# Operands laid out transposed by numpy before the launch, and a new division of U blocks among the stages of a two-layer decoder trunk

## The chip, the cores and the metric

One core of a Trainium2 chip runs the whole program in one launch. The metric is the device time of that launch in microseconds (us). What numpy does to the inputs before the launch is not in the time. The engines are TensorE (PE, with its weight loads shown as PEld), VectorE (DVE), ScalarE (ACT), GpSimd (POOL) and SyncE (SP), which here only issues DMAs.

## What is computed

Two layers (DEPTH 2) over 512 tokens of width 1024. Each layer is a mixing sub-layer (stick-breaking attention, mLSTM, spatial gating) and then a retrieval of experts, which takes most of the time:

```python
q = matmul(xt, wq).reshape(t, 8, 2, 128)
scores = einsum('thcd,hcnd->thcn', q, sub_keys)         # 2 x 128 keys for each of 8 heads
sv, si = top_k(scores, 16)                              # then the 16 best of the 16 x 16 sums: idx, gate
act = einsum('td,thkd->thk', xb, u_tab[idx])            # u_tab: 16384 x 1024
y = einsum('thk,thkd->td', gelu(act) * gate, v_tab[idx])
```

The spatial gating multiplies by `w_s * tril`, four 128x128 matrices in a layer.

## The kernel before, in words

For the first 384 tokens (TD) the kernel doesn't gather experts: it computes the gelu of the products of all 16384 rows of U with the tokens, multiplies by a dense matrix of gates, and multiplies by all rows of V. The tables go through in 128 blocks of 128 rows: a U block e, a V block k. The last 128 tokens are gathered row by row: 256 indirect DMAs of 512 KB in a layer (`gather_u`, `gather_v`), each followed by one DVE product. Every fp32 operand is split in two parts of type fp32r (`u_hi` and `u_lo`, `v_hi` and `v_lo`, `wh` and `wl`), and each product takes three matmuls.

Stages of a layer, in order of time:

1. Front: `mixing` and `peer_front` (L618). For each of 16 pairs of head and half, `peer_front` loads the keys `kr`, turns them on PE (L648), copies them to `kt` on ACT (L650), and multiplies. `sg_all` (L537) turns its four matrices on PE in the same way (L550).
2. Selection: `stage2` (L803) for four tiles of tokens, nearly all of it on DVE.
3. One-hot: `onehots` (L895) builds the dense gates from one-hot products: DVE writes `oeq` (L907) and `oag` (L911), PE multiplies them (L917), ACT evacuates (L920), and a DMA stores them in DRAM (`gd`).
4. Tail: the U blocks left until V may begin.
5. V: for each k of 128, load (`vload`), split (`vprep`) and multiply (`vmm`, 18 matmuls of 512 columns, L997); the other U blocks lie among these.

A U block is 24 matmuls of 384 columns (`uact`, L738), then a gelu on ACT (L741). Before it, `uload` (L683) brings 512 KB of U rows through SP's queue and `utrans` (L693) makes the transposed halves, in one of two ways. In the stages selection and one-hot, eight PE transposes into two PSUM tiles T (L711), then for each tile an ACT copy to `u_hi` (L713) and a DVE subtraction to `u_lo` (L714). From the tail on, for blocks e of at least `u_tail + 3` (L1000), the rows come in four DMAs of 128 KB arranged in 32x32 squares, DVE turns them in one instruction (L702), and then follow one ACT copy (L705) and one DVE subtraction (L706). The tiles `u_hi` and `u_lo` have two buffers each, so block e + 1 is prepared while block e is multiplied, in the buffers of block e - 1; `u_raw` has three.

What divides the U blocks: `paced` (L925) takes the steps of selections and one-hot products, adds a credit for each step (W_S = 1.0 for each of 27 selection steps, W_O / 2 = 0.25 for each of 96 one-hot steps), and emits one U block (`uphase`, L745) for each whole credit. 27 + 24 = 51 blocks are emitted so. The tail takes e from 51 to UB + 2 = 62, 12 blocks, and the V loop the other 65, spread over its first 120 steps (`u_on`). The results of the first NS = 52 blocks are stored in DRAM (`ge`) and read back before their V block (`gelu_r`); later ones stay in NB = 11 buffers. One gather is emitted for every second one-hot step (48), one for each tail block, and the rest are spread over the V loop.

The tail and the V loop lie in a `manual_schedule` block: there each engine's order is the order of the code. Elsewhere a scheduler with a cost model of its own fixes each engine's order when the program is built.

Of the kernel before, what the change touches and what calls it, by code (L numbers as in the profile page):

```python
# [7 lines left out]
F32 = mybir.dt.float32  # L8
F32R = mybir.dt.float32r
# [3 lines left out]
AF = mybir.ActivationFunctionType  # L13
# [4 lines left out]
P = 128  # L18
S = 512
NT = S // P  # L20
D = 1024
ND = D // P
# [10 lines left out]
NK = 128  # L33
# [8 lines left out]
NCH = TD // TC  # L42
GE = 4
GPAD = 128
NB = 11
NS = 52
UB = NS + NB - 3
W_S = 1.0
W_O = 0.5
G_R = 1  # L50
G_B = 1
DVT = 0
UDV = []
GBUF = 4
UEND = 120
LOG_EXP = "natural_log_exp_and_others"
# [12 lines left out]
@with_exitstack  # L69
def trunk_kernel(ctx: ExitStack, tc: tile.TileContext, x, norm1_g, w_in, sb_qn_g, sb_kn_g, ml_conv_w,  # L70
                 ml_conv_b, ml_i_b, ml_f_b, sg_vn_g, sg_w, sg_b, out_g, w_out, norm2_g, peer_wq,
                 peer_keys, peer_u, peer_v, out):
    nc = tc.nc
    depth = w_in.shape[0]

# [4 lines left out]
    ident = consts.tile([P, P], F32, name="ident")  # L80
# [109 lines left out]
    def blocked(ap):  # L190
        return ap.rearrange("p (f c) -> p c f", c=ND)
# [56 lines left out]
    def mixing(l, wst, fr, at, ps):  # L248
# [3 lines left out]
        with ExitStack() as yctx:  # L252
# [284 lines left out]
            def sg_all():  # L537
                sq = tmp("e", 1)[:, :NT * WG].rearrange("p (t g d) -> p t g d", t=NT, d=HD)
                nc.vector.tensor_mul(sq, vv, vv)
                r = small.tile([P, NT, GS], F32, name="sgr")  # L540
                nc.vector.tensor_reduce(r, sq, op=ALU.add, axis=AX.X)
                rsqrt_mean(r, r, HD)
                nc.vector.tensor_mul(vv, vv, r[:, :, :, None].to_broadcast([P, NT, GS, HD]))
                for t in range(NT):
                    nc.vector.tensor_mul(vv[:, t], vv[:, t], vn.rearrange("p (g d) -> p g d", d=HD))
                for g in range(GS):
                    wr = tmp("dg", 2, (P, NT, P))[:, 0, :]
                    nc.sync.dma_start(wr, sg_w[l, g])
                    pw = ps.tile([P, S], F32, name="tr", bufs=1)
                    nc.tensor.transpose(pw[:, :P], wr, ident)  # L550
                    wt = tmp("dg", 2, (P, NT, P))[:, 0, :]
                    nc.vector.tensor_mul(wt, pw[:, :P], upper)
                    pg = ps.tile([P, S], F32, name="tr", bufs=1)
                    pg4 = pg[:, :NT * HD].rearrange("p (t d) -> p t d", d=HD)
                    nc.tensor.matmul(pg4, wt, vv[:, :, g, :], start=True, stop=True)
                    ug = uu[:, :, g * HD:(g + 1) * HD]
                    nc.vector.scalar_tensor_tensor(ug, pg4, col("sgb", g), ug, op0=ALU.add, op1=ALU.mult)
                    sum_sq(ug, rsg[:, :, g])
# [59 lines left out]
    def peer_front(l, pctx, mctx, at, wst, ps, pools, uload):  # L618
# [17 lines left out]
        with ExitStack() as fctx:  # L636
            fr = fctx.enter_context(tc.tile_pool(name="pf", bufs=1, side="right"))
            for c0 in range(0, 2 * PH, 3):
                n = min(3, 2 * PH - c0)
                wn = load_split(wst, peer_wq[l], (c0 + 3) * P, min(3, 2 * PH - c0 - 3) * P,  # L640
                                perm=True) if c0 + 3 < 2 * PH else None
                for c in range(n):
                    hc = c0 + c
                    h, which = hc // 2, hc % 2
                    kr = fr.tile([P, P], F32, name="kr", bufs=2)
                    nc.sync.dma_start(kr, peer_keys[l, h, which])
                    pk = ps.tile([P, S], F32, name="zz", bufs=4)
                    nc.tensor.transpose(pk[:, :P], kr, ident)  # L648
                    kt = fr.tile([P, P], F32, name="kt", bufs=2)
                    nc.scalar.activation(kt, pk[:, :P], AF.Copy)  # L650
                    pt = ps.tile([P, S], F32, name="mm", bufs=2)
                    lh = lambda a, d: a[:, d, c * P:(c + 1) * P]
                    for t0, t1 in ((0, TD), (TD, S)) if hc < 2 else ((0, S),):
# [20 lines left out]

    def layer(l):
        with ExitStack() as pctx:
            pools = {"dvt": set(UDV)}
            uraw, uT, vraw, vT, wT, g4 = {}, {}, {}, {}, {}, {}

            def dve_t(e):  # L680
                return e in pools["dvt"]

            def uload(e):  # L683
                if e < NK and dve_t(e):
                    uraw[e] = pools["up"].tile([P, 4, ND * 32], F32, name="u_raw", bufs=3)
                    rows = peer_u[l, e * NK:(e + 1) * NK, :].rearrange("(g b) (a c) -> a b g c", b=32, a=4)
                    for a in range(4):
                        nc.sync.dma_start(uraw[e][32 * a:32 * (a + 1)], rows[a])
                elif e < NK:
                    uraw[e] = pools["up"].tile([P, D], F32, name="u_raw", bufs=3)  # L690
                    nc.sync.dma_start(uraw[e], peer_u[l, e * NK:(e + 1) * NK, :])

            def utrans(e, half, ps, tag="T", **kw):  # L693
                if e >= NK:
                    return
                if half == 0:
                    uT[e] = (pools["up"].tile([P, ND, P], F32R, name="u_hi"), pools["up"].tile([P, ND, P], F32R, name="u_lo"))
                uh, ul = uT[e]
                if dve_t(e):
                    if half == 0:  # L700
                        uraw[e], src = pools["up"].tile([P, ND, P], F32, name="u_t", bufs=1), uraw[e]
                        nc.vector.transpose(uraw[e].rearrange("p c (g b) -> p g c b", g=4),  # L702
                                            src.rearrange("p g (f c) -> p g c f", f=32))
                    else:
                        nc.scalar.activation(uh, uraw[e], AF.Copy)  # L705
                        nc.vector.tensor_sub(ul, uraw[e], uh.bitcast(F32))  # L706
                    return
                pt = ps.tile([P, S], F32, name=tag, **kw)
                d0 = half * 4
                for d in range(4):  # L710
                    nc.tensor.transpose(pt[:, d * P:(d + 1) * P], blocked(uraw[e])[:, d0 + d], ident)  # L711
                p3 = pt.rearrange("p (d e) -> p d e", e=P)
                nc.scalar.activation(uh[:, d0:d0 + 4, :], p3, AF.Copy)  # L713
                nc.vector.tensor_sub(ul[:, d0:d0 + 4, :], p3, uh[:, d0:d0 + 4, :].bitcast(F32))  # L714

            with ExitStack() as fctx:
                ps = fctx.enter_context(tc.tile_pool(name="ps_f", bufs=1, space=PSUM))
                wst = fctx.enter_context(tc.tile_pool(name="wst", bufs=1))
                mctx = ExitStack()
                fr = mctx.enter_context(tc.tile_pool(name="fr", bufs=1))  # L720
                at = mctx.enter_context(tc.tile_pool(name="at", bufs=1))
                mixing(l, wst, fr, at, ps)
                pr, xg, sbuf, svs, sis = peer_front(l, pctx, mctx, at, wst, ps, pools, uload)
                for half in range(2):
                    utrans(0, half, ps, "y", bufs=1)
            dr = pctx.enter_context(tc.tile_pool(name="dr", bufs=1, space=bass.MemoryType.DRAM))
            gd = dr.tile([NCH, P, NK * TC + GPAD], F32, name="gd")
            ge = dr.tile([NS, P, TD], F32, name="ge")
# [16 lines left out]
            def uphase(e, ps):  # L745
                if e:
                    uload(e + 2)
                utrans(e + 1, 0, ps)
                utrans(e + 1, 1, ps)
                uact(e, ps)  # L750

            idx = pr.tile([P, PH * K], I32, name="idx")
# [191 lines left out]
            with ExitStack() as cctx:  # L944
# [52 lines left out]
                                nc.tensor.matmul(ya[2 * t + half], a[:, tsl], b[:, hs],  # L997
                                                 start=(k == 0 and i == 0), stop=(k == NK - 1 and i == 2))

                pools["dvt"].update(range(u_tail + 3 + DVT, NK))  # L1000
                with tc.manual_schedule():
                    uload(u_tail + 2)
                    for n, e in enumerate(range(u_tail, UB + 3)):
                        uload(e + 3)
                        utrans(e + 1, 0, ps, f"y{2 * n % 6}")
                        utrans(e + 1, 1, ps, f"y{(2 * n + 1) % 6}")
                        gather(G_R)
                        uact(e, ps, bufs=2)
                        if e >= UB + 1:
                            vload(e - UB - 1)  # L1010
                    ya += [ps.tile([P, D // 2], F32, name=f"y{i}") for i in range(2 * (NT - 1))]
                    vprep(0)
                    eu = UB + 3
                    for k in range(NK):
                        u_on = eu < NK and (k + 1) * (NK - NS - NB) >= (eu - NS - NB + 1) * UEND
                        vload(k + 2)
                        if u_on:
                            uload(eu + 3)
                            utrans(eu + 1, 0, ps)
                        vprep(k + 1)  # L1020
                        spread(2 * k, 252)
                        if u_on:
                            uact(eu, ps, bufs=2)
                            utrans(eu + 1, 1, ps)
                            eu += 1
                        vmm(k)
                        spread(2 * k + 1, 252)
# [8 lines left out]
    for t in range(NT):  # L1036
# [1 line left out]


_INS = ["x", "norm1_g", "w_in", "sb_qn_g", "sb_kn_g", "ml_conv_w", "ml_conv_b", "ml_i_b", "ml_f_b",  # L1040
        "sg_vn_g", "sg_w", "sg_b", "out_g", "w_out", "norm2_g", "peer_wq", "peer_keys", "peer_u", "peer_v"]
_OUTS = [((1, S, D), "float32")]


# [21 lines left out]
```

## Time and profile before

| | us |
|---|---|
| median of 3 runs | 3360.24 |
| lowest, highest | 3348.55, 3373.12 |
| the profiled execution | 3358.58 |
| its span, first to last instruction | 3356.9 |
| PE, PEld, DVE, ACT, POOL busy | 3237.4, 2875.2, 2792.9, 1395.2, 652.1 |

The profile is one execution. Busy time is the union of an engine's instructions. Matmuls overlap in the profile (one of 384 columns is shown as 340 ns and the next starts sooner than that), so what PE does in a stretch is read from the starts of its instructions, not from their lengths.

### The profile page before, as it was taken

To read this page: it belongs to the slowest core of one execution; us is meant where nothing else is said; L and a number is where in the kernel's file an instruction comes from. 1 tells how busy PE (TensorE), PEld (TensorE's weight loads), DVE (VectorE), ACT (ScalarE), POOL (GpSimd) and SP (SyncE) were. 2 spreads that over 40 slices of the span, in tenths; PEclk is the share of its full clock that TensorE was granted. 3 is DMA by queue.
4 is the path that set the end of the run, shared out by engine and by line. 5 is a ranking of instruction groups with operands and counts; after the bars stand their busy time and mean duration, and the time that the engine had idled before them with its cause. 6 is when DMAs were issued, how large, how long until landed. Compare 5 with 4: busy or idle time off the path is not lost.

```text
span 3356.9 us, 49064 instructions
## 1 busy us (share of the span) xinstructions
PE 3237.4 (96%) x18400; PEld 2875.2 (86%) x18400; DVE 2792.9 (83%) x4911; ACT 1395.2 (42%) x2142; POOL 652.1 (19%) x563
## 2 busy tenths in 40 slices
PE   8999999999999999999989999999999999999999
PEld 8787899898888888888887778889988888888888
DVE  4757898997888888988847578989978888989888
ACT  4554333664333333333355533336643333333333
POOL 1000003111232232223200000032112222332232
PEclk9999999999999999999999999999999999999999
DMA  4212137777999999999732121377779999999997
GB/s 136 72 33 90 56 121 273 265 282 230 279 296 291 283 292 291 304 297 290 246 112 66 32 90 55 121 271 265 282 233 282 296 289 289 302 301 302 286 290 255
DMA packets 388687, 742.40 MB, mean 221 GB/s; under 512 B 32996, under 2 KB 269600, under 8 KB 385376
## 3 DMA queue, kind: packets, MB, share of 16 engines
q1 hardware_dynamic: 295264, 398.64, 43.1%
q0 software_dynamic: 74752, 269.84, 25.4%
q10 hardware_dynamic: 18432, 70.79, 5.3%
q8 instruction: 144, 2.36, 0.3%
q14 instruction: 95, 0.78, 0.1%
HBM read 666.26 MB, written 72.88 MB: 220 GB/s over the span
## 4 chain that ended last, share of the span: by engine, by line
PE 65%; DVE 13%; DMA 11%; issue 5%; ACT 4%; POOL 1%; SPq 0%; ACTq 0%; DVEq 0%; POOLq 0%
PE y L997 22%; PE act L738 17%; PE mm L187 12%; DMA v_raw<-in_peer_v_dram 8%; PE oh L917 3%; PE mm L533 3%; DVE u_lo L714 2%; DMA u_raw<-in_peer_u_dram 1%; DVE u_t L702 1%; PE T L711 1%; PE zz L367 1%; PE zz L659 1%; PE zz L467 1%; PE y L478 1%; PE y L400 1%
## 5 line engine op out<-in xcount | busy, mean ns | idle before, releaser
L738 PE MATMUL act<-xh,u_lo 128*128 128x384 f32 x2048 | 698.1, 341 | 19.4 <-DVE u_lo L706 19.4
L738 PE MATMUL act<-xh,u_hi 128*128 128x384 f32 x2048 | 705.8, 345 | 11.1 <-ACT u_hi L705 10.7
L738 PE MATMUL act<-xl,u_hi 128*128 128x384 f32 x2048 | 696.7, 340 | 0.0
L997 PE MATMUL y<-v_hi,wh 128*128 128x512 f32 x1536 | 600.0, 391 | 8.8 <-ACT wh L984 8.8
L997 PE MATMUL y<-v_lo,wh 128*128 128x512 f32 x1536 | 600.2, 391 | 1.3 <-DVE v_lo L985 1.2
L997 PE MATMUL y<-v_hi,wl 128*128 128x512 f32 x1536 | 599.2, 390 | 0.0
L983 ACT ACTIVATE v_hi<-v_raw 128x1024 fp32r<-128x1024 f32 x256 | 272.0, 1062 | 742.6 <-DMA v_raw<-in_peer_v_dram 336.0
L985 DVE TENSOR_TENSOR v_lo<-v_raw,v_hi 128x1024 fp32r<-128x1024 f32 x256 | 313.1, 1223 | 146.4 <-ACT v_hi L983 146.2
L738 PEld LDWEIGHTS act<-xh,u_lo 128*128 128x128 f32 x2048 | 388.2, 190 | 26.8 <-DVE u_lo L706 26.8
L738 PEld LDWEIGHTS act<-xh,u_hi 128*128 128x128 f32 x2048 | 388.7, 190 | 24.8 <-ACT u_hi L705 17.3
L738 PEld LDWEIGHTS act<-xl,u_hi 128*128 128x128 f32 x2048 | 388.3, 190 | 4.8
L997 PEld LDWEIGHTS y<-v_hi,wh 128*128 128x128 f32 x1536 | 288.9, 188 | 65.8 <-ACT wh L984 10.7
L997 PEld LDWEIGHTS y<-v_hi,wl 128*128 128x128 f32 x1536 | 289.1, 188 | 62.5 <-DVE wl L986 1.5
L997 PEld LDWEIGHTS y<-v_lo,wh 128*128 128x128 f32 x1536 | 289.0, 188 | 58.0 <-DVE v_lo L985 2.9
L702 DVE STREAM_TRANSPOSE u_t<-u_raw 128x1024 f32<-128x1024 f32 x148 | 327.9, 2215 | 0.1
L765 POOL DMA_INDIRECT rows<-in_peer_u_dram,idx x128 | 150.3, 1174 | 788.1 <-DVE rows L768 412.7
L765 POOL DMA_INDIRECT sbuf<-in_peer_u_dram,idx x128 | 147.8, 1154 | 590.4 <-DVE sbuf L768 468.4
L741 ACT ACTIVATE gelu<-act 128x384 f32<-128x384 f32 x256 | 124.3, 485 | 299.7 <-PE act L738 298.7
L776 POOL DMA_INDIRECT rows<-in_peer_v_dram,idx x128 | 172.4, 1347 | 380.7 <-DVE x_sb L779 355.9
L984 ACT ACTIVATE wh<-wf 128x384 fp32r<-128x384 f32 x256 | 132.7, 518 | 244.9 <-DVE wf L980 244.0
L776 POOL DMA_INDIRECT sbuf<-in_peer_v_dram,idx x128 | 163.5, 1277 | 337.0 <-DVE x_sb L779 313.8
L706 DVE TENSOR_TENSOR u_lo<-u_t,u_hi 128x1024 fp32r<-128x1024 f32 x148 | 181.2, 1224 | 55.5 <-ACT u_hi L705 55.1
(309 smaller groups left out, 5890.1 us busy)
## 6 DMA issues: line engine op xcount, KB each, us to landing
v_raw<-in_peer_v_dram SPq DMA_DIRECT2D x256, 512.0 KB, 12.0
u_raw<-in_peer_u_dram SPq DMA_DIRECT2D x592, 128.0 KB, 11.5
u_raw<-in_peer_u_dram SPq DMA_DIRECT2D x108, 512.0 KB, 4.2
gd<-st ACTq DMA_DIRECT2D x24, 2048.0 KB, 7.3
gt<-gd SPq DMA_DIRECT2D x64, 768.0 KB, 14.0
w_raw<-in_w_in_dram SPq DMA_DIRECT2D x28, 768.0 KB, 4.5
ge<-gelu ACTq DMA_DIRECT2D x104, 192.0 KB, 4.4
gelu_r<-ge SPq DMA_DIRECT2D x104, 192.0 KB, 10.4
```

The costliest lines, as they stand in the source:

```text
L187: nc.tensor.matmul(ps, a_sel(a[ah], d), b_sel(b[bh], d), start=(d == 0 and i == 0), stop=(d == n - 1 and i == 2))
L533: nc.tensor.matmul(pt, yT[ah][:, b, t * P:(t + 1) * P], wo[bh][:, b, hs], start=(b == 0 and m == 0), stop=(b == n - 1 and m == 2))
L702: nc.vector.transpose(uraw[e].rearrange("p c (g b) -> p g c b", g=4), src.rearrange("p g (f c) -> p g c f", f=32))
L706: nc.vector.tensor_sub(ul, uraw[e], uh.bitcast(F32))
L738: nc.tensor.matmul(pa[:, :TD], a[:, d, :], b[:, d, :TD], start=(d == 0 and i == 0), stop=(d == ND - 1 and i == 2))
L741: nc.scalar.activation(gelu[e], pa[:, :TD], AF.Gelu_apprx_tanh)
L765: nc.gpsimd.indirect_dma_start(out=r, out_offset=None, in_=u_rows, in_offset=bass.IndirectOffsetOnAxis(ap=idx[:, p:p + 1], axis=0))
L776: nc.gpsimd.indirect_dma_start(out=r, out_offset=None, in_=v_rows, in_offset=bass.IndirectOffsetOnAxis(ap=idx[:, p:p + 1], axis=0))
L983: nc.scalar.activation(vh, vraw[e], AF.Copy)
L984: nc.scalar.activation(wh, wf, AF.Copy)
L985: nc.vector.tensor_sub(vl, vraw.pop(e), vh.bitcast(F32))
L997: nc.tensor.matmul(ya[2 * t + half], a[:, tsl], b[:, hs], start=(k == 0 and i == 0), stop=(k == NK - 1 and i == 2))
```

## The change

Numpy lays out three inputs before the launch: the four `sg_w` matrices and the keys transposed, and a further input `peer_ut` with each block of U transposed, 4 KB in a row for each partition. `utrans` with both its ways is replaced by `uprep`: one load, one ACT copy and one DVE subtraction for a block, from SBUF. The credits are 1.25 and 0.375, so that 33.75 + 36 = 69.75 are given out and 69 whole blocks are emitted among selections and one-hot products (the bound UB is 70), 4 in the tail (e from 69 to 72) and 55 in the V loop. NS is 60, NB is 13. `peer_u` stays for the gathers.

```diff
-NB = 11
-NS = 52
+NB = 13
+NS = 60
 UB = NS + NB - 3
-W_S = 1.0
-W_O = 0.5
+W_S = 1.25
+W_O = 0.75
...
                     nc.sync.dma_start(wr, sg_w[l, g])
-                    pw = ps.tile([P, S], F32, name="tr", bufs=1)
-                    nc.tensor.transpose(pw[:, :P], wr, ident)
                     wt = tmp("dg", 2, (P, NT, P))[:, 0, :]
-                    nc.vector.tensor_mul(wt, pw[:, :P], upper)
+                    nc.vector.tensor_mul(wt, wr, upper)
...
-                    kr = fr.tile([P, P], F32, name="kr", bufs=2)
-                    nc.sync.dma_start(kr, peer_keys[l, h, which])
-                    pk = ps.tile([P, S], F32, name="zz", bufs=4)
-                    nc.tensor.transpose(pk[:, :P], kr, ident)
-                    kt = fr.tile([P, P], F32, name="kt", bufs=2)
-                    nc.scalar.activation(kt, pk[:, :P], AF.Copy)
+                    kt = fr.tile([P, P], F32, name="kt", bufs=3)
+                    nc.sync.dma_start(kt, peer_keys[l, h, which])
...
-            def utrans(e, half, ps, tag="T", **kw):
...
+            def uload(e):
+                if e < NK:
+                    uraw[e] = pools["up"].tile([P, ND, P], F32, name="u_raw", bufs=3)
+                    nc.sync.dma_start(uraw[e], peer_ut[l, e])
+
+            def uprep(e):
+                if e < NK:
+                    uh = pools["up"].tile([P, ND, P], F32R, name="u_hi")
+                    ul = pools["up"].tile([P, ND, P], F32R, name="u_lo")
+                    src = uraw.pop(e)
+                    nc.scalar.activation(uh, src, AF.Copy)
+                    nc.vector.tensor_sub(ul, src, uh.bitcast(F32))
+                    uT[e] = (uh, ul)
...
             def uphase(e, ps):
                 if e:
                     uload(e + 2)
-                utrans(e + 1, 0, ps)
-                utrans(e + 1, 1, ps)
+                uprep(e + 1)
                 uact(e, ps)
...
                         uload(e + 3)
-                        utrans(e + 1, 0, ps, f"y{2 * n % 6}")
-                        utrans(e + 1, 1, ps, f"y{(2 * n + 1) % 6}")
+                        uprep(e + 1)
                         gather(G_R)
                         uact(e, ps, bufs=2)
...
                             uload(eu + 3)
-                            utrans(eu + 1, 0, ps)
                         vprep(k + 1)
                         spread(2 * k, 252)
                         if u_on:
                             uact(eu, ps, bufs=2)
-                            utrans(eu + 1, 1, ps)
+                            uprep(eu + 1)
                             eu += 1
...
+    inputs["sg_w"] = _np.swapaxes(inputs["sg_w"], 2, 3)
+    inputs["peer_keys"] = _np.swapaxes(inputs["peer_keys"], 3, 4)
+    u = _np.asarray(inputs["peer_u"])
+    inputs["peer_ut"] = u.reshape(u.shape[0], NK, NK, P, ND).transpose(0, 1, 3, 4, 2)
```

## Rows read from the trace of the kernel before

**Rows 1.** The page's first part, all of the span: busy us, share of the span and number of instructions of each engine.

```profile
PE 3237.4 (96%) x18400; PEld 2875.2 (86%) x18400; DVE 2792.9 (83%) x4911; ACT 1395.2 (42%) x2142; POOL 652.1 (19%) x563
```

**Rows 2.** Busy time in stretches: from and to in us from the span's start, length, then busy us and number of instructions of PE, PEld, DVE, ACT and POOL, the granted TensorE clock (1.00 is full speed), the busy share of the DMA engines and GB/s. In order: selection, one-hot, tail and V of the first layer, and V of the second.

```profile
438.00:596.00 158.00, 149.00 (x901) 144.35 (x900) 147.15 (x537) 57.98 (x97) 35.25 (x32) 0.99 0.67 229
596.00:788.00 192.00, 187.53 (x1860) 177.70 (x1861) 185.41 (x205) 128.31 (x161) 28.63 (x21) 0.99 0.75 266
788.00:861.00 73.00, 61.85 (x341) 56.39 (x338) 51.99 (x52) 22.87 (x34) 11.15 (x12) 1.00 0.78 221
861.00:1676.00 815.00, 803.63 (x3863) 707.90 (x3864) 717.38 (x781) 283.07 (x384) 243.78 (x194) 0.99 1.03 289
...
2541.00:3357.00 816.00, 803.89 (x3864) 709.99 (x3863) 718.12 (x782) 284.67 (x384) 240.30 (x192) 0.99 1.02 291
```

**Rows 3.** Groups of PE instructions in the selection, 438 to 596 us: line, operation, out<-in, sizes, number | busy us, mean ns of one | idle time before them and what ended it.

```profile
L738 PE MATMUL act<-xh,u_hi 128*128 128x384 f32 x223 | 78.0, 350 | 0.0
...
L711 PE MATMUL T<-ident,u_raw 128*128 128x128 f32 x224 | 32.7, 284 | 8.7 <-DVE u_lo L714 7.8 <-ACT sc L662 0.7
```

**Rows 4.** The same in the one-hot stage, 596 to 788 us.

```profile
L917 PE MATMUL oh<-oag,oeq 128*128 128x128 bf16 x1151 | 79.1, 221 | 4.6 <-DVE oag L911 3.3 <-ACT st L920 0.8
L738 PE MATMUL act<-xh,u_hi 128*128 128x384 f32 x177 | 62.0, 350 | 0.2 <-ACT u_hi L713 0.2
```

**Rows 5.** The same in the tail, 788 to 861 us.

```profile
L738 PE MATMUL act<-xh,u_hi 128*128 128x384 f32 x104 | 36.0, 346 | 2.1 <-ACT u_hi L705 2.1
```

**Rows 6.** The same in V, 861 to 1676 us.

```profile
L997 PE MATMUL y<-v_hi,wh 128*128 128x512 f32 x768 | 300.1, 391 | 5.1 <-ACT wh L984 5.1
...
L738 PE MATMUL act<-xh,u_lo 128*128 128x384 f32 x520 | 176.4, 339 | 6.3 <-DVE u_lo L706 6.3
L738 PE MATMUL act<-xh,u_hi 128*128 128x384 f32 x520 | 176.3, 339 | 2.8 <-ACT u_hi L705 2.8
```

**Rows 7.** PE in order of time in V: start us, us, engine, line, operation, out<-in, sizes, number. The first matmul of a V block, of the U block behind it, and of the next V block.

```profile
1004.10 0.40 PE L997 MATMUL y<-v_hi,wh 128*128 128x512 f32 x1
...
1008.19 0.34 PE L738 MATMUL act<-xh,u_hi 128*128 128x384 f32 x1
...
1012.38 0.40 PE L997 MATMUL y<-v_hi,wh 128*128 128x512 f32 x1
```

**Rows 8.** The same in the selection: the first matmul of a U block, the eight transposes behind it, and the first of the next U block.

```profile
547.66 0.42 PE L738 MATMUL act<-xh,u_hi 128*128 128x384 f32 x1
...
551.92 1.06 PE L711 MATMUL T<-ident,u_raw 128*128 128x128 f32 x8
552.73 0.42 PE L738 MATMUL act<-xh,u_hi 128*128 128x384 f32 x1
```

**Rows 9.** The same in the one-hot stage: 42 one-hot matmuls and what follows them.

```profile
671.88 2.79 PE L917 MATMUL oh<-oag,oeq 128*128 128x128 bf16 x42
674.47 0.42 PE L738 MATMUL act<-xh,u_hi 128*128 128x384 f32 x1
```

**Rows 10.** The same in the front: the transpose of one set of keys.

```profile
338.73 0.27 PE L648 MATMUL zz<-ident,kr 128*128 128x128 f32 x1
```

**Rows 11.** DVE in order of time in the tail, one round; in brackets idle time and what ended it.

```profile
825.86 2.19 DVE L702 STREAM_TRANSPOSE u_t<-u_raw 128x1024 f32<-128x1024 f32 x1
829.24 1.22 DVE L706 TENSOR_TENSOR u_lo<-u_t,u_hi 128x1024 fp32r<-128x1024 f32 x1 [1.19 <-ACT u_hi L705]
830.38 1.22 DVE L768 SCALAR_TENSOR_TENSOR rows<-rows,xg 128x1024 f32<-128x1024 f32 x1
...
831.52 2.18 DVE L702 STREAM_TRANSPOSE u_t<-u_raw 128x1024 f32<-128x1024 f32 x1
```

**Rows 12.** PE where the tail ends: the first matmul of V, and in brackets what it waited for.

```profile
860.96 0.50 PE L997 MATMUL y<-v_hi,wh 128*128 128x512 f32 x1 [3.74 <-ACT wh L984]
```

**Rows 13.** Groups of instructions over all of the span, columns as in rows 3.

```profile
L706 DVE TENSOR_TENSOR u_lo<-u_t,u_hi 128x1024 fp32r<-128x1024 f32 x148 | 181.2, 1224 | 55.5 <-ACT u_hi L705 55.1
...
L911 DVE TENSOR_TENSOR oag<-oeq,gateT 128x2048 bf16<-128x2048 bf16 x144 | 171.3, 1217 | 2.2 <-PE oh L917 2.2
...
L705 ACT ACTIVATE u_hi<-u_t 128x1024 fp32r<-128x1024 f32 x148 | 155.7, 1052 | 71.3 <-DVE u_t L702 71.3
...
L741 ACT ACTIVATE gelu<-act 128x384 f32<-128x384 f32 x256 | 124.3, 485 | 299.7 <-PE act L738 298.7 <-ACT st L920 0.8
...
L859 DVE TENSOR_TENSOR eq<-abb,iota_ak 128x4096 bf16<-128x4096 bf16 x8 | 18.3, 2290 | 0.0
```

**Rows 14.** Busy time and number of line 714 alone (the subtraction behind a PE transpose) in the selection and the one-hot stage: length, DVE busy.

```profile
438.00:596.00 158.00, 35.06 (x55) 0.99 0.67 229
596.00:788.00 192.00, 29.68 (x46) 0.99 0.75 266
```

**Rows 15.** DMA in V, 861 to 1676 us: GB/s in 40 slices of the stretch, packets and bytes, and two kinds of issue with their number, KB each and median us from issue to landing.

```profile
GB/s 287 319 277 293 312 287 302 273 292 285 297 285 286 305 265 268 296 296 331 284 303 287 282 295 289 296 314 295 298 302 301 291 297 304 271 285 318 264 271 152
DMA packets 137409, 235.43 MB, mean 289 GB/s; under 512 B 10420, under 2 KB 96440, under 8 KB 137355
...
v_raw<-in_peer_v_dram SPq DMA_DIRECT2D x125, 512.0 KB, 12.4
u_raw<-in_peer_u_dram SPq DMA_DIRECT2D x248, 128.0 KB, 12.2
```

**Rows 16.** Who waited for whom in V, longest in total first: us in total, times, longest us.

```profile
ACT v_hi L983 <- DMA v_raw<-in_peer_v_dram: 210.5, 51, 9.2
```

More of the change, by code (lines that the diff above doesn't have):

```diff
@@ L44 @@
 GPAD = 128
-NB = 11
-NS = 52
+NB = 13
+NS = 60
 UB = NS + NB - 3
-W_S = 1.0
-W_O = 0.5
+W_S = 1.25
+W_O = 0.75
 G_R = 1
 G_B = 1
-DVT = 0
-UDV = []
 GBUF = 4
@@ L71, in trunk_kernel @@
                  ml_conv_b, ml_i_b, ml_f_b, sg_vn_g, sg_w, sg_b, out_g, w_out, norm2_g, peer_wq,
-                 peer_keys, peer_u, peer_v, out):
+                 peer_keys, peer_u, peer_v, peer_ut, out):
     nc = tc.nc
@@ L676, in layer @@
         with ExitStack() as pctx:
-            pools = {"dvt": set(UDV)}
+            pools = {}
             uraw, uT, vraw, vT, wT, g4 = {}, {}, {}, {}, {}, {}
-            def dve_t(e):
-                return e in pools["dvt"]
             def uload(e):
[L684 to L691, printed above, removed]
@@ L693, in utrans @@
-            def utrans(e, half, ps, tag="T", **kw):
[L694 to L714, printed above, removed]
@@ L723, in layer @@
                 pr, xg, sbuf, svs, sis = peer_front(l, pctx, mctx, at, wst, ps, pools, uload)
-                for half in range(2):
-                    utrans(0, half, ps, "y", bufs=1)
+                uprep(0)
             dr = pctx.enter_context(tc.tile_pool(name="dr", bufs=1, space=bass.MemoryType.DRAM))
@@ L998, in vmm @@
                                                  start=(k == 0 and i == 0), stop=(k == NK - 1 and i == 2))
-                pools["dvt"].update(range(u_tail + 3 + DVT, NK))
                 with tc.manual_schedule():
                     uload(u_tail + 2)
-                    for n, e in enumerate(range(u_tail, UB + 3)):
+                    for e in range(u_tail, UB + 3):
                         uload(e + 3)
-                        utrans(e + 1, 0, ps, f"y{2 * n % 6}")
-                        utrans(e + 1, 1, ps, f"y{(2 * n + 1) % 6}")
+                        uprep(e + 1)
                         gather(G_R)
@@ L1040 @@
 _INS = ["x", "norm1_g", "w_in", "sb_qn_g", "sb_kn_g", "ml_conv_w", "ml_conv_b", "ml_i_b", "ml_f_b",
-        "sg_vn_g", "sg_w", "sg_b", "out_g", "w_out", "norm2_g", "peer_wq", "peer_keys", "peer_u", "peer_v"]
+        "sg_vn_g", "sg_w", "sg_b", "out_g", "w_out", "norm2_g", "peer_wq", "peer_keys", "peer_u", "peer_v", "peer_ut"]
 _OUTS = [((1, S, D), "float32")]
@@ L1053 @@
     arrays, args = {}, []
+    inputs = dict(inputs)
+    inputs["sg_w"] = _np.swapaxes(inputs["sg_w"], 2, 3)
+    inputs["peer_keys"] = _np.swapaxes(inputs["peer_keys"], 3, 4)
+    u = _np.asarray(inputs["peer_u"])
+    inputs["peer_ut"] = u.reshape(u.shape[0], NK, NK, P, ND).transpose(0, 1, 3, 4, 2)
     for name in _INS:
```

## The prediction

> **What bounds the kernel now.** I read the page's first part, then the stretches by stage, then the starts of PE's instructions, because busy PE is no proof: a matmul of 384 columns is shown as 340 ns, and the next starts earlier. The page gives PE 96% and DVE 83% of the span [rows 1]. By stage the first layer has 438 us of front, 158 of selection, 192 of one-hot, 73 of tail and 815 of V; V of the second layer takes 816 [rows 2].
>
> What PE needs in each comes from start to start. In V a V block takes 1008.19 - 1004.10 = 4.09 us and a U block 1012.38 - 1008.19 = 4.19 [rows 7]. Eight transposes take 552.73 - 551.92 = 0.81, and a U block with them 552.73 - 547.66 = 5.07 [rows 8]. 42 one-hot matmuls take 2.59, so 0.062 each [rows 9]. Counts come from the groups, at 8 matmuls of each of three kinds for a U block:
>
> - Selection: 223 / 8 = 27.9 blocks [rows 3] x 5.07 = 141 of 158 us, 17 left as waits.
> - One-hot: 177 / 8 = 22.1 blocks x 5.07 + 1151 x 0.062 [rows 4] = 112 + 71 = 183 of 192, 9 left.
> - Tail: 104 / 8 = 13 blocks [rows 5] x 4.19, with 3 sets of transposes (2.4), = 57 of 73, 16 left.
> - V: 128 x 4.09 + 65 x 4.19 = 523.5 + 272.4 = 796 of 815, 19 left [rows 6].
>
> So PE sets the time nearly everywhere behind the front. DVE is close: 147 of 158 us and 185 of 192 in selection and one-hot, 717 of 815 in V [rows 2]. Only the tail has another bound. There DVE goes round in 831.52 - 825.86 = 5.66 us: the transpose 2.19, 1.19 idle for the ACT copy, the subtraction, a gather's product [rows 11].
>
> [...]
>
> **The change, part by part, for one layer.**
>
> *Front.* 16 key transposes and 4 of sg_w go, with their copies. One is shown as 0.27 us [rows 10]; 20 x 0.27 = 5 us is the upper end, zero the lower, since DVE is busy with top-k there. I take 2: 436.
>
> *Selection and one-hot.* They now emit 69 whole U blocks (69.75 credits) instead of 51. PE: 69 x 4.19 + 71 = 289 + 71 = 360, and 1 for the nine transposes of stage2: 361. DVE: before 147 + 185 = 332; the subtractions behind PE transposes took 35.1 + 29.7 = 65 of it [rows 14]. The new one is the tail's form, 1.22 us shown and 830.38 - 829.24 = 1.14 to the next start [rows 11, 13]: 69 x 1.14 = 79. So 332 - 65 + 79 = 346, less than PE's 361 but near it. ACT has 58 + 128 of 350 us before [rows 2]; a copy of 1.05 [rows 13] and a gelu of 0.49 for 69 blocks leave it far from full.
>
> What is late next is the chain that refills a buffer. Block e + 1 goes into the buffers of e - 1, so when PE ends e - 1: gelu 0.49, copy 1.05, subtraction 1.22 [rows 13], with handovers of 0.1 each about 3.0 us. PE meanwhile does e in 4.19. The slack is 1.2 us. An instruction of 2.29 (L859) or 1.22 (L911) [rows 13] ahead on DVE uses it up, so some waits stay. Before, the two stages had 17 + 9 = 26 us of waits, 7.8 of them transposes waiting for a free PSUM tile [rows 3], which go. Bounds: none, and 26 again plus 18/51 of it, 35. I take 17: 361 + 17 = 378.
>
> *Tail.* 4 blocks, no DVE transpose. DVE then has a subtraction and a gather's product, 2.3 us for a block, so PE sets the pace: 4 x 4.19 = 17. At its end V's first matmul waited 3.7 us for `wh` [rows 12], because the first loads are issued only two blocks before. That stays. The gates of the last one-hot chunk must now be stored and read back within 5 blocks, 21 us, instead of 13; a load of V takes 12.4 to land [rows 15]. I take 6 us of waits, bounds 2 and 20: 23.
>
> *V.* 128 x 4.09 + 55 x 4.19 = 523.5 + 230.5 = 754. DVE loses 65 transposes of 2.2, so it goes from 717 to about 570 busy and is no more the cause of waits. PE's waits there were on `u_lo` 6.3, `wh` 5.1 and `u_hi` 2.8 [rows 6]. I take 15 of 19 as staying, bounds 5 and 30: 769.
>
> *DMA.* U blocks come in one load with 4 KB in a row instead of four with 1 KB. V's bytes: 235.4 MB now [rows 15], less 10 U blocks (-5.2), plus 8 gathers moved from the tail (+4.2) and 8 more results read back (+1.6): 236, over 769 us 307 GB/s. The slices of V reach 331, 319 and 318 [rows 15], so I cost this at nothing. Cover for it: V loads are issued about two V periods ahead. ACT already waits 210 us for them [rows 16], while PE hardly does.
>
> [...] No row here goes over 331.
>
> **The sum.** 436 + 378 + 23 + 769 = 1606 us for the layer, before 1676: 70 less. The second layer has the same stages within a microsecond or two [rows 2], so 140. The profiled execution took 3358.6: 3218. It stands 1.7 below the median of the runs, 3360.24, so the same figure serves for that. The three runs spread by 0.4% to either side; about 1% is what a measurement can tell from no change.
>
> **The rivals.**
>
> 1. *DMA sets V.* For: 289 GB/s as a mean with engines at a share of 1.03 [rows 2], and the ACT waits. Against: higher slices, and larger pieces for U. If 289 is a ceiling, 236 MB take 817 us, V gains nothing, the layer is 436 + 378 + 23 + 817 = 1654, 22 less: 3315.
> 2. *The buffer chain in selection and one-hot (slower).* If the scheduler's order puts every subtraction behind a batch of five one-hot products, 5 x 1.14 = 5.7 us, the chain is 3.0 + 5.7 = 8.7. With two buffers the period of a block is (4.19 + 8.7) / 2 = 6.45 instead of 4.19, 69 x 2.26 = 156 us in place of the 17: the layer is 1606 - 17 + 156 = 1745, 69 more: 3497. It decides from where a block loses (70 + 17) / 69 = 1.26 us. For: DVE is 93 to 97% busy there, and its order was made by a cost model. Against: 51 blocks lost 26 us before, 0.5 each.
> 3. *The removed work was covered.* If PE waited as long for DVE and ACT as its transposes took, the blocks only change place: 3359. For: DVE at 185 of 192. Against: a period of 5.07 without idle time in rows 8.
> 4. *Better.* No waits in selection, one-hot and V's loop: 436 + 361 + 23 + 754 = 1574, 102 less: 3155.
>
> **How the numbers follow.** My forecast 0.70 (its own range 3170 to 3265 from the bounds of the waits), rival 1 0.13, rival 2 0.05, rival 3 0.05, rival 4 0.07. Faster by over 1%: 0.70 + 0.13 + 0.07 = 0.90; within 1%: rival 3, 0.05; slower: rival 2, 0.05. Predicted 3218; for 8 in 10 the range goes from rival 4, 3155, up to 3300, which takes in a half of what rival 1 would cost.
>
> **What would show it.** L711, L702 and L648 gone. V near 769 with 4.19 and 4.09 unchanged. A tail of about 23. Selection and one-hot together near 378, with PE waits on `u_lo` under 20. Wrong would be: V over 800 with ACT and PE waiting for `v_raw` (rival 1); PE waits on `u_lo` of over 80 us in the two stages (rival 2); a gap of over 20 us in front of V.

## The result, and the profile after

The changed kernel took 3236.91 us (median of 4 runs, 3232.98 to 3247.25), the kernel before, measured beside it, 3363.49: a ratio of 0.9632, 95% interval 0.9589 to 0.9675. The prediction was 3218 (3155 to 3300, faster with 0.90). The profiled execution is the longest of the four, 3247.25 us, with a span of 3245.5.

The page's first part after, against [rows 1]: PE lost 95 us, DVE 312. The 148 DVE transposes that went, at 2.19 each [rows 11, 13], come to 324 by themselves.

```profile
PE 3142.2 (97%) x17496; PEld 2784.1 (86%) x17496; DVE 2480.4 (76%) x4655; ACT 1381.0 (43%) x2002; POOL 679.9 (21%) x563
```

The stretches of the first layer after, columns as in [rows 2]: selection, one-hot, tail, V.

```profile
447.00:619.00 172.00, 154.19 (x830) 150.18 (x831) 154.12 (x518) 61.99 (x82) 50.07 (x33) 0.95 0.69 235
619.00:845.00 226.00, 224.04 (x1990) 209.31 (x1988) 196.90 (x192) 146.38 (x164) 33.68 (x19) 0.98 0.71 256
845.00:867.50 22.50, 18.77 (x100) 18.28 (x97) 10.10 (x14) 8.13 (x12) 3.82 (x4) 0.92 0.84 310
867.50:1623.00 755.50, 755.11 (x3624) 663.89 (x3624) 584.02 (x723) 270.79 (x364) 244.19 (x201) 1.00 0.91 312
```

V is now PE from end to end (755.11 of 755.50), at a DMA share of 0.91 where it was 1.03. The selection is the opposite: PE is busy for 154 of 172 us, at a granted clock of 0.95 where it was 0.99 [rows 2]. With stage lengths from the starts of PE's instructions:

| us in a layer | before, layer 1 / 2 | predicted | after, layer 1 / 2 |
|---|---|---|---|
| front | 439.6 / 443.1 | 436 | 447.2 / 441.8 |
| selection + one-hot | 348.4 / 348.0 | 378 | 397.8 / 397.9 |
| tail | 73.0 / 73.3 | 23 | 22.6 / 22.5 |
| V | 815.2 / 811.4 | 769 | 755.3 / 755.5 |
| sum | 1676.2 / 1675.9 | 1606 | 1622.8 / 1617.6 |

The gain of about 111 us between the two profiled executions came from tail and V; selection and one-hot grew by 50 a layer. There are two misses of opposite sign: V is 14 us a layer better than predicted, selection and one-hot 20 worse. The experiments look for both causes.

PE in order of time after, columns as in [rows 7]. The first five rows are the worst wait of the selection, the last two a U block in V.

```profile
581.20 0.34 PE L707 MATMUL act<-xl,u_hi 128*128 128x384 f32 x1
586.58 0.69 PE L707 MATMUL act<-xh,u_lo 128*128 128x384 f32 x1 [5.05 <-DVE u_lo L683]
587.07 0.52 PE L707 MATMUL act<-xh,u_hi 128*128 128x384 f32 x1
...
591.55 0.41 PE L707 MATMUL act<-xh,u_lo 128*128 128x384 f32 x1
591.80 0.34 PE L707 MATMUL act<-xh,u_hi 128*128 128x384 f32 x1
...
1005.67 0.34 PE L707 MATMUL act<-xh,u_hi 128*128 128x384 f32 x1
...
1009.86 0.40 PE L965 MATMUL y<-v_hi,wh 128*128 128x512 f32 x1
```

In V a U block still takes 1009.86 - 1005.67 = 4.19 us. In the selection PE stands 5.05 us for `u_lo`, and then its matmuls start 0.32 us apart (587.07 to 591.55 in 14 steps), where 0.175 is the pace of V (4.19 / 24). From 586.58 to 591.80, 16 steps take 5.22 us instead of 2.8. The granted clock from 586.5 to 592.0 is 0.53, and 0.175 / 0.53 = 0.33, so the fall of the clock adds 2.4 us to a wait of 5.

DVE at the same time, after: it stood 2.22 and 2.52 us for the rows of a gather, and the subtraction for PE came only behind.

```profile
580.41 1.23 DVE L736 SCALAR_TENSOR_TENSOR rows<-rows,xg 128x1024 f32<-128x1024 f32 x1 [2.22 <-DMA rows<-in_peer_u_dram,idx]
...
584.16 1.22 DVE L736 SCALAR_TENSOR_TENSOR rows<-rows,xg 128x1024 f32<-128x1024 f32 x1 [2.52 <-DMA rows<-in_peer_u_dram,idx]
585.31 0.08 DVE L736 DVE_READ_ACCUMULATOR rows<-rows,xg 128x1 f32 x1
585.31 1.22 DVE L683 TENSOR_TENSOR u_lo<-u_raw,u_hi 128x1024 fp32r<-128x1024 f32 x1
```

Who waited for whom after (total us, times, longest): two rows of the selection (447 to 619), then V's largest of PE (867 to 1623).

```profile
PE act L707 <- DVE u_lo L683: 13.3, 7, 5.1
DVE rows L736 <- DMA rows<-in_peer_u_dram,idx: 13.8, 9, 3.2
...
PE y L965 <- ACT wh L952: 1.9, 1, 1.9
```

Of the 13.3 us of waits for `u_lo`, 3.5 lie before the first gather product of the stage (539 us) and 9.9 behind it, in 4 waits.

Two theories for the selection: **A**, gather products queued ahead of `u_lo` wait for their data; **B**, DVE simply has too much to do there. Three for V: **C**, the DVE transposes had held it back; **D**, the loads of U in 1 KB pieces; **E**, those loads because each DMA wrote only a quarter of the partitions.

### The profile page after: what moved, and what is told of

Read it like the earlier page. It is cut to its first block, busy times and chain, and to the rows that moved or that the text cites. A ratio compares the mean times of both kernels' runs of the same rounds, so it can differ in the third digit from the quotient of the medians.

```text
span 3245.5 us, 46361 instructions
## 1 busy us (share of the span) xinstructions
PE 3142.2 (97%) x17496; PEld 2784.1 (86%) x17496; DVE 2480.4 (76%) x4655; ACT 1381.0 (43%) x2002; POOL 679.9 (21%) x563
## 4 chain that ended last, share of the span: by engine, by line
PE 81%; DVE 10%; issue 3%; ACT 3%; POOL 2%; DMA 1%; SPq 0%; POOLq 0%; DVEq 0%; ACTq 0%
PE y L965 32%; PE act L707 23%; PE mm L185 13%; PE oh L885 3%; PE mm L531 3%; DVE u_lo L683 2%; DVE oag L879 1%; PE zz L365 1%; POOL rows L733 1%; PE zz L651 1%; PE zz L465 1%; PE y L476 1%; PE y L398 1%; PE zz L390 1%; POOL sbuf L733 1%
## 5 line engine op out<-in xcount | busy, mean ns | idle before, releaser
L683 DVE TENSOR_TENSOR u_lo<-u_raw,u_hi 128x1024 fp32r<-128x1024 f32 x256 | 310.8, 1221 | 222.5 <-ACT u_hi L682 219.7
L682 ACT ACTIVATE u_hi<-u_raw 128x1024 fp32r<-128x1024 f32 x256 | 270.6, 1058 | 268.5 <-PE act L707 262.9
L733 POOL DMA_INDIRECT sbuf<-in_peer_u_dram,idx x128 | 176.6, 1380 | 672.7 <-DVE sbuf L736 552.2
L733 POOL DMA_INDIRECT rows<-in_peer_u_dram,idx x128 | 176.2, 1376 | 639.3 <-DVE c L794 353.6
L710 ACT ACTIVATE gelu<-act 128x384 f32<-128x384 f32 x256 | 124.2, 485 | 284.2 <-PE act L707 283.8
L888 ACT ACTIVATE st<-oh 128x512 f32<-128x512 f32 x192 | 203.9, 1145 | 86.9 <-PE oh L885 86.9
L744 POOL DMA_INDIRECT rows<-in_peer_v_dram,idx x128 | 151.4, 1182 | 317.9 <-DVE x_sb L747 295.9
```

The source lines that it names most:

```text
L682: nc.scalar.activation(uh, src, AF.Copy)
L683: nc.vector.tensor_sub(ul, src, uh.bitcast(F32))
L710: nc.scalar.activation(gelu[e], pa[:, :TD], AF.Gelu_apprx_tanh)
L733: nc.gpsimd.indirect_dma_start(out=r, out_offset=None, in_=u_rows, in_offset=bass.IndirectOffsetOnAxis(ap=idx[:, p:p + 1], axis=0))
L744: nc.gpsimd.indirect_dma_start(out=r, out_offset=None, in_=v_rows, in_offset=bass.IndirectOffsetOnAxis(ap=idx[:, p:p + 1], axis=0))
L888: nc.scalar.activation(st[:, :, o:o + 4].rearrange("p i t -> p t i"), pg, AF.Copy)
```

## The experiments

Edits are on the changed kernel unless said otherwise. Medians are of 4 runs, and ratios go against the kernel before, measured beside each. "sel+oh" is selection and one-hot together, first layer. The expectations have letters of their own: in e3, e4 and e7 their theory C is A here and their rival D stands against it; in e5, e6, e9 and e10 their F and F2 are C here; their E is D here in e5 and e6, and E2 is E here.

**Layout alone (e1).**

```diff
-NB = 13
-NS = 60
+NB = 11
+NS = 52
-W_S = 1.25
-W_O = 0.75
+W_S = 1.0
+W_O = 0.5
```

> The changed kernel with the old division of U blocks: NB 11, NS 52, W_S 1.0, W_O 0.5, so 51 blocks among selections and one-hot products, 12 in the tail, 65 in V. Theory A (the removed transposes give most of it, as the sum said): selection and one-hot of a layer about 340 us (PE 51 x 4.19 + 72 = 286, DVE 332 - 65 + 58 = 325 and some waits), tail 56, V 797, front 442, layer 1635: about 3275 us, so 85 of the 127 us gained. Theory B (the division is what counts, and the transposes lay in PE's waits): selection and one-hot stay near 350, tail 70, V 815: 3350.

3263.84 us, 0.9719 (0.9667 to 0.9771). V took 798.4 with 65 U blocks, where PE needs 796 by the same sum as before: the layout alone took 17 of V's 19 us of waits. sel+oh took 332.5 us, 15.9 less than before, though 51 x (5.07 - 4.19) = 45 us of transposes had gone from PE. In the one-hot stage DVE is the bound now, 199.48 of 201 us (stretch 572 to 773):

```profile
572.00:773.00 201.00, 178.78 (x1683) 163.16 (x1683) 199.48 (x211) 124.16 (x140) 57.08 (x35) 0.97 0.77 290
```

**New division alone (e2), on the kernel before.** The four constants of the change, nothing else.

```diff
-NB = 11
+NB = 13
-NS = 52
+NS = 60
-W_S = 1.0
-W_O = 0.5
+W_S = 1.25
+W_O = 0.75
```

> The kernel before with the new division alone: NB 13, NS 60, W_S 1.25, W_O 0.75, transposes as before. Theory A: selection and one-hot 69 x 5.07 + 72 = 422 and about 30 us of waits, tail 27, V 769, front 441: layer 1689, about 3385 us, no gain or slightly slower than before. Theory B: selection and one-hot near 400, V 755: about 3260.

3417.82 us, 1.0177 (1.0124 to 1.0231): slower by 1.2 to 2.3%, and 33 us more than expected, most of it in V (782.5 us, where 769 was expected). So the layout gives 98 us of the gain (3361.52 - 3263.84), the division 27 more on top of it (3263.84 - 3236.91, not measured side by side), but 56 of loss without it. In the first layer sel+oh grew by 108, and tail and V fell by 48 and 33. An early block costs PE 5.07 us there and 4.19 in V, and waits were added in both places: PE on DVE in the selection (438 to 643), PE on ACT in V (919 to 1702).

```profile
PE T L711 <- DVE u_lo L714: 18.7, 12, 4.5
...
PE y L997 <- ACT wh L984: 15.3, 9, 4.4
```

V has the changed kernel's 55 U blocks in 782.5 us instead of 755: 754 needed, 28 lost. That is the clearest pair for the question of V.

**A third buffer for `u_hi` and `u_lo` (e3).**

```diff
-                    uh = pools["up"].tile([P, ND, P], F32R, name="u_hi")
-                    ul = pools["up"].tile([P, ND, P], F32R, name="u_lo")
+                    uh = pools["up"].tile([P, ND, P], F32R, name="u_hi", bufs=3)
+                    ul = pools["up"].tile([P, ND, P], F32R, name="u_lo", bufs=3)
```

> The changed kernel with three buffers for u_hi and u_lo instead of two, so that a block can be prepared one block of PE (4.2 us) earlier. Theory C (in the selection the subtraction u_lo stands on DVE behind gather products that wait for their DMA, up to 5 us, and with two buffers PE has only about 1.2 us of slack): the waits of the two stages, about 37 us in a layer, fall to about 12, and the granted clock there rises from 0.95: about 3190 us. Rival D (DVE has simply too much to do in the two stages, 351 of 398 us): the stages stay at about 398 and the time near 3237.

3215.23 us, 0.9568 (0.9518 to 0.9618): less of a gain than expected. sel+oh fell from 397.8 to 388.8 us only. A third buffer gives a block more of slack, 4.19 us. Why it gave no more stays open. One reading, not tried by itself, is that a DVE queue which stops for one gather after another uses that up. Another is late loads: in this selection ACT's copies waited 33.9 us (7 times) for U blocks, in the changed kernel not once.

**No gathers among the one-hot steps (e4).** They move to the V loop.

```diff
-G_B = 1
+G_B = 0
```

> The changed kernel with no gathers emitted among the one-hot steps (G_B 0): all but 4 of the 256 gathers of a layer go to the V loop. Theory C: without gather products on DVE the waits in selection and one-hot fall from 37 to about 12 us a layer. V then carries 236 + 25 = 261 MB: if 331 GB/s is its ceiling it grows from 755 to about 789 and the sum is near 3255; if PE still sets it (755), near 3185. Rival D (the chain through two buffers alone makes the waits): selection stays near 170 us.

3207.22 us, 0.9548 (0.9498 to 0.9599). That is 22 us more than theory C had expected with PE setting V (3185). sel+oh took 377.4 us, 20.4 less. PE's waits for `u_lo` in the selection are 4.1 us, about the 3.5 that lay before any gather product. V had the 48 gathers more and took 758. Its stretches (selection, then V) and its DMAs in V:

```profile
445.00:596.00 151.00, 145.79 (x812) 143.13 (x813) 121.06 (x459) 60.50 (x79) 5.87 (x4) 0.98 0.53 168
...
845.00:1603.00 758.00, 756.76 (x3622) 663.28 (x3622) 637.41 (x818) 273.96 (x364) 323.48 (x249) 1.00 0.96 344
```

```profile
GB/s 359 348 361 290 388 376 323 363 344 378 340 312 393 335 371 354 343 367 310 364 382 318 321 386 353 351 333 349 363 371 322 388 328 364 350 334 338 274 351 164
DMA packets 118310, 260.71 MB, mean 344 GB/s; under 512 B 8308, under 2 KB 63604, under 8 KB 118261
```

V carries 344 GB/s with PE at 756.76 of 758. The prediction's rival 1, a ceiling at 289 GB/s, falls.

**The same DVE work without the data to wait for (e7).** No gathers among one-hot steps, and in their place a product of `xg` with itself.

```diff
-                        gather(G_B * (n % 2))
+                        if n % 2:
+                            nc.vector.scalar_tensor_tensor(dum, xg, 1.0, xg, op0=ALU.mult, op1=ALU.mult,
+                                                           accum_out=dacc[:, n:n + 1])
```

> As the run with the gathers late, but with 48 DVE products of the same size in a layer in the gathers' place among the one-hot steps, on a tile that is already there (their results are not used). Theory C (PE waits because u_lo stands behind products that wait for their DMA): the selection stays near 152 us, the one-hot stage near 226 to 232, about 3210 to 3225. Rival D (the mere work of the products, 48 x 1.2 us on DVE): selection back near 171, about 3245.

3212.03 us, 0.9583 (0.9557 to 0.9609); sel+oh 379.5 us. The scheduler put 30 of the 48 products into the selection, about where the gathers' 29 had been, and they waited for nothing (groups of DVE, 440 to 600 us, columns as in [rows 3]):

```profile
L683 DVE TENSOR_TENSOR u_lo<-u_raw,u_hi 128x1024 fp32r<-128x1024 f32 x33 | 40.1, 1219 | 3.2 <-ACT u_hi L682 3.1
L912 DVE SCALAR_TENSOR_TENSOR dum<-xg 128x1024 f32<-128x1024 f32 x30 | 36.6, 1221 | 0.4
```

The work costs 2 us of sel+oh (379.5 against 377.4), the gathers with their waits 20.4. DVE is as busy in the two stages as in the changed kernel, 350 against 351 us. That is A, not B. What it doesn't separate: the gathers' traffic is gone too, and with it any slowing of other loads. In the changed kernel ACT waited for no U load in these two stages, so the traffic did not hold up `u_lo` by that way.

**Both at once (e8): G_B = 0 and the third buffer.**

> Both at once, the gathers late and three buffers for u_hi and u_lo. With gathers late the selection has 11 and the one-hot stage 5 us of waits a layer left, most of them on u_lo; three buffers took 11 a layer off the changed kernel. Expected: 5 to 9 a layer less than the gathers late alone, 3190 to 3198. If the three buffers only covered the waits for gathers, 3207 as without them.

3186.33 us, 0.9506 (0.948 to 0.9532), a little better than expected and than both kernels, 1.3% below the changed one by the ratios (0.9506 / 0.9632). sel+oh took 368.5 us and the selection's clock is 1.00 (selection, one-hot, tail, V):

```profile
442.00:587.00 145.00, 142.35 (x812) 141.06 (x813) 120.83 (x459) 60.60 (x80) 6.39 (x4) 1.00 0.54 175
587.00:811.00 224.00, 222.52 (x2007) 210.07 (x2005) 177.24 (x156) 147.49 (x166) 0.94 (x1) 1.00 0.60 215
811.00:831.00 20.00, 16.91 (x96) 16.59 (x96) 7.91 (x11) 7.31 (x11) 2.88 (x3) 1.00 0.80 303
831.00:1590.00 759.00, 757.88 (x3624) 663.72 (x3624) 638.71 (x819) 273.73 (x365) 323.50 (x249) 1.00 0.96 344
```

**A DVE transpose for each U block, its result unused (e6).**

```diff
+                    if e > UB + 3:
+                        ut = pools["up"].tile([P, ND, P], F32, name="u_t", bufs=1)
+                        flat = src.rearrange("p c e -> p (c e)")
+                        nc.vector.transpose(ut.rearrange("p c (g b) -> p g c b", g=4),
+                                            flat.rearrange("p (g f c) -> p g c f", g=4, f=32))
```

> The changed kernel with a DVE transpose of 2.2 us for each U block of the V loop from number 74 on, into a tile that nobody reads: DVE in V goes from 584 to about 703 of 755 us. Rival F: V goes up by 10 to 28 us a layer, 3257 to 3290. Theory E: V stays near 755, about 3240.

3230.53 us, 0.9643 (0.9616 to 0.9669). V took 755.1: DVE's work as such costs nothing there.

**The transpose in the chain (e10).** It runs ahead of the ACT copy and the subtraction, where the kernel before had it.

```diff
+            def uturn(e):
...
+                    nc.vector.transpose(uraw[e].rearrange("p c (g b) -> p g c b", g=4),
+                                        src.rearrange("p g (f c) -> p g c f", f=32))
...
+                            uturn(eu + 1)
                         vprep(k + 1)
```

> The changed kernel with its one load, and in the V loop a DVE transpose of each U block at the place where the kernel before had it, ahead of V's products on DVE, and in the chain, its result going into u_hi and u_lo (so these blocks are turned once too often). Rival F2: V goes up by 15 to 30 us a layer, 3267 to 3300. Theory E2: V stays near 755, about 3240.

3235.68 us, 0.9637 (0.9606 to 0.9668). Its stretch V, columns as in [rows 2]:

```profile
861.50:1617.00 755.50, 755.45 (x3622) 664.14 (x3623) 693.45 (x776) 271.54 (x364) 251.21 (x201) 1.00 0.91 311
```

DVE has 693 us, as in e2, and V stays at 755.5. C falls in both its forms.

**U blocks in four DMAs of 1 KB pieces, each to all 128 partitions (e5).**

```diff
-                    nc.sync.dma_start(uraw[e], peer_ut[l, e])
+                    for a in range(0, ND, 2):
+                        nc.sync.dma_start(uraw[e][:, a:a + 2, :], peer_ut[l, e, :, a:a + 2, :])
```

> The changed kernel, each U block loaded in four DMAs of 128 KB with pieces of 1 KB, as the kernel before did, and nothing else. Theory E (V's waits before came from the small pieces: loads landed in 12 us instead of less, and the copies of V came late): V, 755 us with no waits in the changed kernel, goes back up by 10 to 28 us a layer, 3257 to 3290, with v_raw landing in about 12 us. Rival F (they came from DVE's transposes): V stays 755, about 3237.

3238.37 us, 0.9658 (0.9625 to 0.9692), V 756.4. D falls.

**The load of the kernel before, without the transpose (e9).**

```diff
+                        rows = peer_u[l, e * NK:(e + 1) * NK, :].rearrange("(g b) (a c) -> a b g c", b=32, a=4)
...
+                        for a in range(4):
+                            nc.sync.dma_start(flat[32 * a:32 * (a + 1)], rows[a])
```

> The changed kernel, where blocks from 72 on are loaded exactly as in the kernel before: four DMAs, each of 32 partitions, in pieces of 1 KB, and not turned afterwards (so the U products of these blocks use rows that are not transposed). Theory E2 (not the size of the pieces but this form of load, a quarter of the partitions at a time, slows all of V's DMAs): V goes from 755 to 770 to 785 us a layer, 3267 to 3300, v_raw landing near 12 us. Rival F2 (only DVE's transpose standing in front of V's own DVE work does it): V stays 755, about 3237.

3283.33 us, 0.9784 (0.9735 to 0.9832), V 776.9 and 773.2: 20 us a layer are back. ACT waits for V's loads as it did before [rows 16]. Its wait in V, 860 to 1637 (total us, times, longest):

```profile
ACT v_hi L957 <- DMA v_raw<-in_peer_v_dram: 229.2, 56, 9.6
```

And these loads take as long as before [rows 15], by the DMA issues of the same stretch:

```profile
v_raw<-in_peer_v_dram SPq DMA_DIRECT2D x125, 512.0 KB, 12.7
```

In e4, with more bytes, the same loads land in 6.7 us, and in the changed kernel ACT waits 1.0 us for them in V.

**Load and transpose (e11).** The diffs of e9 and e10 together; blocks 72 and 73 are loaded in the old way but not turned.

> Both at once: V's U blocks loaded and turned as in the kernel before, under the new division of blocks. If these two are all that made V's waits before, V comes to 780 to 785 us as in the run with the division alone, about 3295. If V stays under 765, a third thing is missing.

3283.59 us, 0.9778 (0.9744 to 0.9812), V 785.4 and 784.1: the 782.5 and 784.6 of e2 are made up again, and no third thing is needed. V is 8.5 and 10.9 us longer than in e9, in one profiled execution of each. The medians of e9 and e11 are the same, so that the transpose costs something where the loads are late is not shown.

**Quarter loads from the new table (e12).** The same pieces as in e5, four DMAs a block, but each into 32 partitions.

```diff
+                        for a in range(4):
+                            src = peer_ut[l, e - 3:e + 1, 32 * a:32 * (a + 1), 2 * a:2 * a + 2, :]
+                            nc.sync.dma_start(flat[32 * a:32 * (a + 1)], src.rearrange("g p c x -> p g (c x)"))
```

> From block 72 on, each U block is loaded from the transposed table in four DMAs of 128 pieces of 1 KB, each DMA into 32 partitions; the pieces of a block are taken from it and the three blocks before it (other numbers, the same count of bytes and pieces), so the output of these blocks is not the reference's. Against e5 only the partitions that one DMA writes differ (32 instead of 128); against e9 only the table and the order in which it is read. If writing a quarter of the partitions with each DMA is what made the loads slow in e9: V 773 to 780 us, v_raw landing in about 12 us, 3275 to 3290. If it is the order in which the table is read: V 755 to 758, 3230 to 3245.

3278.03 us, 0.9779 (0.9726 to 0.9831), V 778.8 and 772.4: as e9. Two tables, read in different orders, are slow when each DMA writes 32 partitions (V 776.9 and 778.8 us), and the new one is not when each writes 128 (756.4 in e5); that is E. What goes with it is not separated: in e12 a partition takes its four pieces of a block in one DMA, and they come from four blocks of the table. The stretch V of e5, and in it the queue that SP feeds (q1) and the queue of the gathers (q0), each with packets, MB, and the time of its packets as a share of 16 engines:

```profile
859.00:1615.00 756.00, 755.95 (x3623) 664.60 (x3624) 583.57 (x723) 270.79 (x364) 244.24 (x201) 1.00 0.92 312
```

```profile
q1 hardware_dynamic: 104967, 129.91, 52.3%
q0 software_dynamic: 28944, 105.39, 39.5%
```

The same of e12, and ACT's wait for the loads of V, which is 2.5 us in e5:

```profile
860.50:1639.50 779.00, 766.94 (x3624) 665.53 (x3624) 582.88 (x723) 268.75 (x365) 271.74 (x201) 0.99 1.02 303
```

```profile
q1 hardware_dynamic: 104936, 129.76, 60.9%
q0 software_dynamic: 28944, 105.39, 41.1%
...
ACT v_hi L957 <- DMA v_raw<-in_peer_v_dram: 241.3, 55, 12.4
```

Packets and bytes are the same; the time on q1 goes from 0.523 x 756 = 395 to 0.609 x 779 = 474 us, 79 more, and on q0 from 299 to 320, 21 more. In this stretch the packets of 1 KB on q1 are the 52 U blocks' alone, 27.3 MB. By the packet records of the two traces they take 82.6 us of engine time in e5 and 124.2 in e12, 50 and 75 ns each, so the quarter loads take 1.5 times as long as the same bytes to 128 partitions. These are 42 of the 79 us. The other 37 and the 21 on q0 fall on loads that did not change: their packets took 12% longer on q1 and 7% on q0. So the 16 engines come to the share that V had before, 1.02 here and 1.03 there [rows 2].

Why a DMA into 32 partitions takes 1.5 times the engine time for the same bytes, no row here shows.

## Why the prediction was right, and where it was off

*The path.* PE sets V in both kernels, and the sum of 4.09 and 4.19 us a block came out within 2 us. Rival 3 (covered work) is out for the time as a whole, since the layout alone gave 98 us. In the selection and the one-hot stage it was true in part at the old division: 45 us of PE transposes went there and the stages fell by 15.9 us, with DVE as the bound of the one-hot stage (e1). It is the new division that put U blocks into the PE time set free.

*The measure of headroom.* Weight loads fill 663.89 of V's 755.50 us, 88%, where the starts leave 1 us. By the weight loads 12% of V would be open, by the starts next to nothing. Here the starts decide: V took 755.3 us, and the sum from the starts is 754.

*Front, 436.* This was not borne out. With the same front it took 437.6 to 447.2 us from one execution to the next and layer to layer, so a gain of 2 can't be seen. The profiled execution lies 10 us over the median; its front of 447.2 is the longest seen and may be part of that.

*Selection and one-hot, 378.* The term "17 of waits" was mis-sized. Whole blocks in the two stages were 69 as predicted, so PE needs 361; 397.8 - 361 = 37 were lost, just over the upper bound of 35. The selection alone lost 171.7 - (34.1 x 4.19 + 1) = 28. What the trace shows as PE's waits is not far from 17: 18.3 us in the selection (13.3 for `u_lo`, 3.4 for the `oag` of the first one-hot product, 1.6 for others) and 1.6 in the one-hot stage. The sum had no term for the clock. The granted clock was 0.95 over the 172 us of the selection and 0.98 over the 226 of the one-hot stage, 0.99 in both before [rows 2]; 0.05 x 172 + 0.02 x 226 = 13 us is an upper estimate of its cost, since PE stood for a part of the slow time. Some 4 us or more are left without a cause. So the sign "PE waits on `u_lo` under 20" held, and the stages missed the forecast all the same.

What stands behind most of the waits, and the fall of the clock with them (0.95 in the selection, 0.98 without these gathers in e4), is missing from the prediction's list of what may stand ahead of `u_lo` on DVE: the list had long instructions in it, but not an instruction that waits. The scheduler had put 29 gather products into the selection, where they waited 13.8 us for rows; the kernel before had 28 of them there already. Without them the stages fell by 20.4 us (e4), and with products that wait for nothing in their place by 18.3 (e7). Rival 2, a subtraction behind a batch of one-hot products, did not come: in the one-hot stage PE waited on `oag`, not on `u_lo`.

*Tail, 23.* It took 22.6 and 22.5 us. PE's waits in it were 1.8 us on `st` and, at V's first matmul, 1.9 on `wh`, where the prediction had 3.7 for `wh` as staying; the granted clock of 0.92 makes up most of the rest, 0.08 x 22.5 = 1.8 us as an upper estimate. The total of 6 was right, its parts were not.

*V, 769.* The sum for PE, 754, is right; "15 of 19 as staying" is wrong, about 1 stayed. The edit that took them away is the one of which the prediction said "I cost this at nothing": the load of U. With quarter loads ACT gets `v_raw` late and hands its waits on to PE (e9: ACT waits 229.2 us, and V is 20 us longer). The reasoning behind it compared GB/s and piece sizes, and neither was the limit (344 GB/s in e4, 1 KB pieces in e5); V's loads came late where the DMA engines' share was 1.03 [rows 2], with ACT waiting 210.5 us for them [rows 16]. As e9 (1.03) and e12 (1.02) show, that share belongs to the quarter loads; at 0.91, where ACT waited 1.0 us, and at 0.96 in e4, where they landed in 6.7 us, V's loads come in time. Rival 1 had taken the right sign, an engine share over 1, for a ceiling on bytes.

*The sum.* V gave 14 us a layer more than predicted, selection and one-hot took 20 more, the front 6 to 11 more. So a total within 19 us of the forecast rests partly on errors that cancel, which is luck; the mechanism was right for PE, the two wait terms were not. Two smaller slips are in the working. The second layer was taken as equal to the first within a microsecond or two; by the starts its V before was 811.4 us, 4 less, since the row of 816 us runs 5 us past the last product. And the upper end of the range, 3300, takes in 82 of the 97 us that rival 1 would cost, not a half.

Left open are the part of the gathers' cost that is their traffic rather than their wait (e7 takes both), and the 5 to 10 us by which fronts differ.

## What to carry to other kernels

In the order of an engine's instructions, look for those that wait for a DMA ahead of the one that feeds the critical engine: here such products held DVE up to 3.2 us at a time and PE up to 5.1, and 30 products of the same length that waited for nothing cost 2 us. Where loads land late at a DMA share like the 1.02 and 1.03 here, with fewer GB/s (303 and 289) than the 344 that ran in time at 0.96, look for the limit in engine time, not in bytes, and ask which loads use that time badly; here loads written 32 partitions at a time took 1.5 times the engine time of the same bytes to 128, and the other loads beside them 7 to 12% more. And divide work anew only after the price of a unit has changed in the stages concerned: the same division was worth -27 us on the new layout and +56 on the old.

## What the runs showed of the hardware

- Four DMAs of 128 KB in 1 KB pieces cost nothing against one of 512 KB in 4 KB pieces when each wrote all 128 partitions (V 756 and 755 us), and 23 us in the first layer and 17 in the second when each wrote 32 (e12 against e5). The packets of these loads took 75 ns of engine time instead of 50.
- With one core active, V carried 344 GB/s on the mean and up to 393 in a slice (e4). V before had 289 on the mean and 331 at most [rows 15]; neither was a ceiling.
- A PE wait of 5.05 us was followed by 16 matmuls at about 0.32 us instead of 0.175, at a granted clock of 0.53: 2.4 us on top of the wait.
